# Second products of the feed-forward blocks: three ScalarE casts ordered behind the copy of the first product's bank

## The chip, the cores and the metric

The kernel runs on one core of a Trainium2 chip. The metric is the device time of one execution in microseconds (us); smaller is better. TensorE multiplies, ScalarE and VectorE prepare operands and read results, SyncE issues nearly all transfers, GpSimd does little here. Each engine works through its own list of instructions in the order in which the built program holds them.

## The reference, cut to what matters

Two layers of a streaming-encoder trunk over 256 rows of 1024 channels, in float32. Each layer is a feed-forward block, a mixer (a convolution in the first layer, latent attention in the second) and another feed-forward block, so there are four feed-forward blocks in all:

```python
def swiglu_ffn(h, w1, w3, w2):
    return (jax.nn.silu(h @ w1) * (h @ w3)) @ w2

for i in range(DEPTH):                       # 2 layers, D_FF = 2816
    h = h + 0.5 * swiglu_ffn(rmsnorm(h, ffn_norm1[i]), ffn1_w1[i], ffn1_w3[i], ffn1_w2[i])
    m = rmsnorm(h, mix_norm[i])
    ...
    h = h + 0.5 * swiglu_ffn(rmsnorm(h, ffn_norm2[i]), ffn2_w1[i], ffn2_w3[i], ffn2_w2[i])
```

The change touches only the last product of each block, (...) @ w2, called the down product here.

## The kernel before

**Split operands.** Every float32 operand of a matmul is split in two: a high part, which is ScalarE's cast of the value to the format fp32r, and a low part, which is VectorE's subtraction value minus high part. `mm3` (L330 to L336) makes one product of three matmuls: high times low weight (L332), high times high (L335) and low times high (L336). In the profile a matmul `o<-lo,Gh` is that of L332, `o<-hi,Gl` that of L336.

**Up and gate.** A feed-forward block (`ffn_in`, L834) runs six chunks of the 2816 hidden columns, five of 512 and a sixth of 256. For each chunk and each half of the rows (`tb` 0 and 1) ScalarE computes silu (L948), VectorE multiplies with the other product (L950), and `turn` (L838) brings the gate into transposed form: VectorE transposes 32x32 squares (L470), SyncE writes them to DRAM in four transfers (L474, `gd<-gt`) and reads them back (L479, `gb<-gd`), ScalarE casts them into `Gh` and VectorE subtracts into `Gl` (both L845). `turn` keeps each pair of cast and subtraction in the list `gates`, two pairs a chunk. The first two chunks' gates are read back into the tile `rows4`, since their sums are needed too.

**Seven products in place of eight.** The first 1024 of the hidden columns are multiplied by a scheme that needs seven block products instead of eight (`seven_products`, L366). It wants four sums of row blocks and seven combinations of weight blocks. `sums_of_rows` (L338) makes the sums in `rows4`; `forms_of` (L352) splits each sum into a high part (ScalarE, L361) and a low part (VectorE, L362). The first sum's parts (`s1h`, `s1l`) are made early, ahead of the last chunk; the other three are made when the down product begins (L955), and their parts lie in the space of the block's input (tiles `Xh` and `Xl`, in the profile `rows<-rows`). `load_seven` (L189) makes the weight combinations: differences of raw blocks on VectorE (L200, `raw<-raw,raw`), ScalarE casts (L214) and VectorE subtractions (L200, `lo<-raw,hi`), the last two in halves of 1024 columns.

The products are called P1 to P7 here, each of 12 matmuls:

| product | rows | into bank | waits for |
|---|---|---|---|
| P1 | gate rows | c11 | weights |
| P2 | sum 0 (`s1h`, `s1l`) | c22 | weights |
| P3 | sum 1 | c21, which holds a copy of c11 after P1 | the copy (L383, ScalarE `o<-o`) |
| P4 | gate rows | c11 | weights |
| P5 | sum 2 | c21 | the addition c12 = c21 + kept (L388, VectorE `o<-o,p`), which reads c21 after P3 |
| P6 | sum 3 | c12 | weights |
| P7 | gate rows | c21 | the second addition, c22 = c21 + kept (L395) |

`kept` is ScalarE's copy of c22 after P2 (L386, in the profile `p<-o`). Copies and additions pass through `urgent`, so that in the profile they all stand at L258. P7's weights need a weight difference (`raw<-raw,raw`) that `load_seven` puts behind P5's parts, then a cast, then a subtraction.

**What sets the order.** The instructions are not placed by hand: a scheduler at build time puts them in order, engine by engine, by the position in the program, by priority (`urgent` raises it), by the dependencies of tiles, and by a model of when each could run. `order(ins, first)` (L154) adds an edge between two instructions: `ins` stands behind `first`. L389 to L392 and L396 use it already for the last chunk's gates and for two weight subtractions. When `seven_products` runs for the down product, `gates` ends with the two pairs of the sixth chunk (256 columns); the entry before them is the second half of the fifth chunk.

In the first feed-forward block ScalarE also makes the diagonals of the coming convolution (L1667, `rows<-dpair,wpair`); they are written over `rows4` and so wait until the sums there have been split.

The four down products are called stages A, B, C and D here: A ends the first feed-forward block (126 to 147 us), B the second (399 to 415), C the third (576 to 592), D the fourth (842 to 858).

Of the kernel before, what the change touches and what calls it, by code (L numbers as in the profile page):

```python
# [22 lines left out]
NT = S // P  # L23
# [66 lines left out]
def trunk(ctx: ExitStack, tc: tile.TileContext, x, xt, first, pos, invf, gfin, wdw,  # L90
          f1w13, f1w2, f2w13, f2w2, cw1, cw2, wa, wuq, wukv, wo, wpair, out):
    nc = tc.nc
# [12 lines left out]
    def uid(s):  # L105
        n_uid[0] += 1
        return f"{s}_{n_uid[0]}"
# [9 lines left out]
    def seven(four):  # L117

        group = {}
        return [("seven", j, four, group) for j in range(7)]  # L120
# [33 lines left out]
    def order(ins, first):  # L154
        tc.add_manual_dep(ins.ins, first.name, mybir.DependencyInfo(
            mybir.DependencyClass.NoSync, mybir.DependencyReason.DATA), reason="order")
# [95 lines left out]
    def urgent(f):  # L252

        def g(*args, **kw):
            traced = nc.cur_bb.bb.instructions
            n = len(traced)
            with tc.high_priority():
                r = f(*args, **kw)  # L258
            last = {ins.engine: ins for ins in traced[n:]}
            for engine, ins in last.items():  # L260
                ahead_of.setdefault(engine, []).append(ins)
            return r
        return g

    def load_ahead(ahead=W_BUFS - 2):
        load_to(min(len(blocks), n_used[0] + ahead))
# [5 lines left out]
    def weights(n=1, more=True):  # L272
        out = []
        for _ in range(n):
            n_used[0] += 1
            if more:
                load_ahead()
            else:
                load_ahead(0)
            out.append(loaded[n_used[0] - 1])  # L280
        return out
# [48 lines left out]
    def mm3(o, ah, al, bh, bl, start, stop, after=(), seeded=False):  # L330

        mm = nc.tensor.matmul(o, ah, bl, start=start, stop=False, skip_group_check=seeded)  # L332
        for a in after:
            order(mm, a.ins)
        nc.tensor.matmul(o, ah, bh, start=False, stop=False, skip_group_check=seeded)  # L335
        return nc.tensor.matmul(o, al, bh, start=False, stop=stop, skip_group_check=seeded)  # L336

    def sums_of_rows(x11, x12, x21, x22):  # L338


        sums = [(0, x22, x21, x22, ALU.add), (2, x21, x11, x21, ALU.subtract), (1, x11, x22, x11, ALU.subtract),
                (3, x12, x12, x11, ALU.subtract)]
        for n, out, left, right, op in sums:
            nc.vector.tensor_tensor(out, left, right, op=op)
        return sorted(((n, out) for n, out, *_ in sums), key=lambda s: s[0])

    def whole_rows(xh, xl):
        x = rawp.tile([P, HB], F32, tag="raw", name=uid("xs")).rearrange("p (k t) -> p k t", t=S)
        nc.vector.tensor_add(x, xh.bitcast(F32), xl.bitcast(F32))
        return [x[:, 4 * a:4 * a + 4, tbs(tb)] for tb in range(2) for a in range(2)]  # L350

    def forms_of(sums, sh, sl):  # L352
        sh, sl = (z.rearrange("p k t -> p (k t)").rearrange("p (n c) -> p n c", c=512) for z in (sh, sl))
        out = {}
        for i, (n, x) in enumerate(sums):
            if len(x.shape) == 2:
                high, low = (z[:, i].rearrange("p (t i q) -> p t i q", t=4, q=32) for z in (sh, sl))
                x = x.rearrange("p (i t q) -> p t i q", i=4, q=32)
            else:
                high, low = (z[:, i].rearrange("p (k t) -> p k t", t=P) for z in (sh, sl))  # L360
            nc.scalar.copy(high, x)  # L361
            nc.vector.tensor_sub(low, x, high.bitcast(F32))  # L362
            out[n] = [z[:, i].rearrange("p (k t) -> p k t", t=P) for z in (sh, sl)]
        return out

    def seven_products(xh, xl, forms, banks):  # L366


        def rows(a, tb):
            k = slice(4 * a, 4 * a + 4)  # L370
            return xh[:, k, tbs(tb)], xl[:, k, tbs(tb)]

        def product(a, b, fresh):
            load_ahead(W_BUFS - 1)
            (hi, lo), = weights(1, False)
            for k in range(4):
                c = slice(k * 512, k * 512 + 512)
                mm3(b, a[0][:, k], a[1][:, k], hi[:, c], lo[:, c], fresh and k == 0, k == 3, (), True)

        n0 = n_used[0]  # L380
        c11, c21, c12, c22 = banks[0, 0], banks[1, 0], banks[0, 1], banks[1, 1]
        product(rows(0, 0), c11, True)
        urgent(nc.scalar.copy)(c21, c11)  # L383
        product(forms[0], c22, True)
        kept = tmp.tile([P, 512], F32, tag="s", name=uid("p5"))
        last = urgent(nc.scalar.copy)(kept, c22)  # L386
        product(forms[1], c21, False)
        add = urgent(nc.vector.tensor_add)(c12, c21, kept)  # L388
        order(casts[n0 + 5, 0][1], add.ins)  # L389
        for high, low in gates[-NT:]:  # L390
            order(high, last.ins)
            order(low, add.ins)  # L392
        product(rows(1, 0), c11, False)
        product(forms[2], c21, False)
        add = urgent(nc.vector.tensor_add)(c22, c21, kept)  # L395
        order(casts[n0 + 6, 0][1], add.ins)  # L396
        product(forms[3], c12, False)
        product(rows(1, 1), c21, False)
# [8 lines left out]
    def tbs(tb):  # L407
        return slice(tb * P, (tb + 1) * P)
# [336 lines left out]
    class Rows:  # L745
# [3 lines left out]
                                                      ((0, 0), (0, 1), (1, 0), (1, 1)))}  # L749
            self.seeded = seeded  # L750

        def seven(self, forms):
            seven_products(self.zh, self.zl, forms, self.o)

        def mm(self, part, i, tb, d, o, f0, f1, o0=0, o1=512, after=(), after_last=()):
            hi, lo = part
# [69 lines left out]
    gates = []  # L826

    def ffn(X, make_next, beside=lambda: None, apart=False):
        n = n_ffns[0]
        n_ffns[0] += 1  # L830
        with tc.tile_pool(name=uid("ffn"), bufs=1) as act:
            return ffn_in(act, X, make_next, beside, apart, SEVEN_UP.get(n, ()), n in SEVEN_DOWN)

    def ffn_in(act, X, make_next, beside, apart, seven_up, seven_down):  # L834
        first_form = {}
# [40 lines left out]
        for c in range(6):  # L876

            both = c == 5
# [5 lines left out]
            if seven_up and c == min(seven_up) - (1 if X.whole else 2):  # L884
                forms = forms_of(sums_of_rows(*whole_rows(X.xh, X.xl)), Gh[:, 14:], Gl[:, 14:])
            if c in seven_up:
                for key in ((0, 0), (0, 1), (1, 1), (1, 0)):
                    u[key] = bank("A", "u")
                seven_products(X.xh, X.xl, forms, {(tb, m): b for (m, tb), b in u.items()})
                beside()  # L890
                beside()
            if both and seven_down:
                z11, z21, z12, z22 = (rows4[:, n, :] for n in range(4))
                down_sums = sums_of_rows(z11, z12, z21, z22)
                first_form = forms_of(down_sums[:1], *(act.tile([P, 2, S], F32R, tag=tag, name=uid(tag))
                                                       for tag in ("s1h", "s1l")))
# [55 lines left out]
        o = Rows(Gh, Gl, NF, make_next is Final, seven_down)  # L952
        if seven_down:
            both = (xp.tile([P, KT, S], F32R, tag=tag, name=uid("rows")) for tag in ("Xh", "Xl"))
            o.seven({**first_form, **forms_of(down_sums[1:], *both)})  # L955
        stage.append("down")
        for i in range(4 if seven_down else 0, NF // 2 - (3 if apart else 2)):
            beside()
# [717 lines left out]
    class Rows512:  # L1676

        n = {"ht": 0, "hb": 0}
# [128 lines left out]
```

## Time and profile before

| what | value |
|---|---|
| median of 3 runs | 900.82 us (898.79 to 901.63) |
| the profiled execution's own time | 902.66 us |
| its span (first to last instruction) | 900.9 us |
| granted TensorE clock over it | 0.998 |
| TensorE busy | 890.0 us, 99% of the span |
| VectorE busy | 743.2 us, 83% |
| ScalarE busy | 571.8 us, 63% |

A row of a timeline gives the start in us from the start of the span, the duration, the engine, the line, the operation with out<-in, its shape and count; in brackets stands the idle time of the engine just before it and what ended that. A row of waits gives the engine and its line, what it waited for, the total in us, how often, and the longest. TensorE's matmuls overlap: one is shown as 0.39 us long, while the next starts before it has ended.

### The profile page before, as it was taken

Reading aid. Unit: us, or ns where it says so; the run is one execution under the profiler, and the core shown is the slowest. Engines: PE = TensorE matmul, PEld = TensorE weight load, DVE = VectorE, ACT = ScalarE, POOL = GpSimd, SP = SyncE. Lnnn points to the kernel's source line nnn. Section 1 sums busy time; section 2 is a strip of 40 time slices with the busy share of each in tenths; the row PEclk is TensorE's granted clock in tenths of the full one; section 3 lists DMA queues with packets and bytes.
Section 4 is the critical chain, followed back from the end, with each engine's and each line's share of the span. In section 5 each row is a group of like instructions: output and inputs, shape, how many; then the busy total and the mean of one; then the engine's idle time right before and its main releaser. Section 6 shows DMA issues by size and latency. Waiting matters only on the chain.

```text
span 900.9 us, 12238 instructions
## 1 busy us (share of the span) xinstructions
PE 890.0 (99%) x4221; PEld 745.7 (83%) x4221; DVE 743.2 (83%) x1083; ACT 571.8 (63%) x993; POOL 104.9 (12%) x227
## 2 busy tenths in 40 slices
PE   9999999999999999999999999999999999999997
PEld 7888887898988888878888888788899888888886
DVE  6787779579998998899588989994768579999963
ACT  7966468388877645666375566564767576374752
POOL 1000000069962000000010000000400010000000
PEclk9999999999999999999999999999999999999999
DMA  9987629734315864939759369396545449377451
GB/s 333 363 313 282 212 69 335 295 125 171 105 57 207 291 241 154 368 98 356 283 167 331 136 206 354 98 384 219 198 165 178 150 141 352 99 287 293 169 200 47
DMA packets 71054, 198.94 MB, mean 221 GB/s; under 512 B 12368, under 2 KB 41936, under 8 KB 51664
## 3 DMA queue, kind: packets, MB, share of 16 engines
q1 hardware_dynamic: 70560, 197.47, 61.2%
q8 instruction: 33, 0.54, 0.2%
q10 hardware_dynamic: 432, 0.69, 0.2%
q14 instruction: 29, 0.24, 0.1%
HBM read 181.87 MB, written 16.25 MB: 220 GB/s over the span
## 4 chain that ended last, share of the span: by engine, by line
PE 82%; DVE 7%; DMA 6%; ACT 2%; issue 2%; SPq 0%; POOL 0%; DVEq 0%; ACTq 0%
PE u L336 13%; PE u L332 13%; PE u L335 13%; PE o L332 8%; PE o L336 8%; PE o L335 8%; PE u L993 3%; PE gate L993 3%; DVE lo L200 3%; DMA raw<-in_f1w 2%; PE u L403 2%; PE o L1229 2%; DMA raw<-in_f2w 2%; DVE raw L200 2%; DMA gd<-gt 1%
## 5 line engine op out<-in xcount | busy, mean ns | idle before, releaser
L247 DVE TENSOR_TENSOR lo<-raw,hi 128x1024 fp32r<-128x1024 f32 (+1 forms) x236 | 276.5, 1213 | 41.7 <-ACT hi L246 40.4
L246 ACT CAST hi<-raw 128x1024 fp32r<-128x1024 f32 (+1 forms) x238 | 236.5, 1044 | 89.1 <-DMA raw<-in_f2w 25.1
L332 PE MATMUL u<-lo,Xh 128*128 128x512 f32 x612 | 238.9, 390 | 0.3
L335 PE MATMUL u<-hi,Xh 128*128 128x512 f32 x612 | 238.4, 390 | 0.0
L336 PE MATMUL u<-hi,Xl 128*128 128x512 f32 x612 | 238.2, 390 | 0.0
L332 PEld LDWEIGHTS u<-lo,Xh 128*128 128x128 f32 x612 | 115.0, 188 | 25.3 <-DVE lo L200 1.6
L336 PEld LDWEIGHTS u<-hi,Xl 128*128 128x128 f32 x612 | 115.0, 188 | 24.5 <-DVE Xl L457 0.4
L335 PEld LDWEIGHTS u<-hi,Xh 128*128 128x128 f32 x612 | 115.0, 188 | 23.7
L214 ACT CAST hi<-raw 128x1024 fp32r<-128x1024 f32 x98 | 97.8, 1051 | 53.3 <-DVE raw L200 44.8
L200 DVE TENSOR_TENSOR lo<-raw,hi 128x1024 fp32r<-128x1024 f32 x98 | 116.0, 1217 | 6.4 <-ACT hi L214 6.3
L332 PE MATMUL o<-lo,Gh 128*128 128x512 f32 (+1 forms) x276 | 106.5, 388 | 0.4 <-DVE lo L200 0.4
L335 PE MATMUL o<-hi,Gh 128*128 128x512 f32 (+1 forms) x276 | 106.7, 387 | 0.0
L336 PE MATMUL o<-hi,Gl 128*128 128x512 f32 (+1 forms) x276 | 106.5, 386 | 0.0
L429 POOL TENSOR_TENSOR ms<-ss 128x1 f32<-128x1 f32 x16 | 8.1, 510 | 603.9 <-ACT junk L421 603.9
L200 DVE TENSOR_TENSOR raw<-raw,raw 128x2048 f32<-128x2048 f32 x28 | 63.8, 2280 | 3.9 <-DMA raw<-in_f2w 1.9
L332 PEld LDWEIGHTS o<-lo,Gh 128*128 128x128 f32 x276 | 51.9, 188 | 11.6 <-DVE lo L200 1.3
L336 PEld LDWEIGHTS o<-hi,Gl 128*128 128x128 f32 x276 | 51.9, 188 | 10.5
L335 PEld LDWEIGHTS o<-hi,Gh 128*128 128x128 f32 x276 | 51.9, 188 | 10.3
L1082 DVE SCALAR_TENSOR_TENSOR acc<-V,dw,acc 128x128 f32<-128x128 f32 (+1 forms) x174 | 53.9, 392 | 0.0
L1103 ACT ACTIVATE prod<-V,dw 128x128 f32<-128x128 f32 (+1 forms) x128 | 45.5, 415 | 1.8 <-POOL Y L1104 1.0
L845 ACT CAST Gh<-gb 128x512 fp32r<-128x512 f32 (+1 forms) x32 | 18.1, 567 | 39.2 <-DMA gb<-gd 39.2
L789 DVE SCALAR_TENSOR_TENSOR h<-o,rh,h 128x512 f32<-128x512 f32 (+1 forms) x18 | 12.9, 719 | 29.6 <-PE o L336 29.6
(265 smaller groups left out, 1274.6 us busy)
## 6 DMA issues: line engine op xcount, KB each, us to landing
raw<-in_f2w SPq DMA_DIRECT2D x66, 1024.0 KB, 6.3
raw<-in_f1w SPq DMA_DIRECT2D x62, 1024.0 KB, 6.6
raw<-in_cw SPq DMA_DIRECT2D x12, 1024.0 KB, 5.0
gd<-gt SPq DMA_DIRECT2D x160, 64.0 KB, 3.0
gb<-gd SPq DMA_DIRECT2D x24, 256.0 KB, 2.8
rows<-gd SPq DMA_DIRECT2D x16, 256.0 KB, 4.7
raw<-in_wo SPq DMA_DIRECT2D x4, 1024.0 KB, 4.8
hd<-rows SPq DMA_DIRECT2D x56, 64.0 KB, 2.2
```

The costliest lines, as they stand in the source:

```text
L200: ins = nc.vector.tensor_sub(out, left, right)
L214: casts[n, i] = nc.scalar.copy(hi[:, c], raw[:, c]), sub(lo[:, c], raw[:, c], hi[:, c].bitcast(F32))
L246: casts[len(loaded), i] = (nc.scalar.copy(hi[:, c], raw[:, c]), low.tensor_sub(lo[:, c], raw[:, c], hi[:, c].bitcast(F32)))
L247: low.tensor_sub(lo[:, c], raw[:, c], hi[:, c].bitcast(F32)))
L332: mm = nc.tensor.matmul(o, ah, bl, start=start, stop=False, skip_group_check=seeded)
L335: nc.tensor.matmul(o, ah, bh, start=False, stop=False, skip_group_check=seeded)
L336: return nc.tensor.matmul(o, al, bh, start=False, stop=stop, skip_group_check=seeded)
L403: mm = nc.tensor.matmul(o, al if kind == "x" else ah, bl if kind == "l" else bh, start=start and n == 0, stop=stop and n == len(kinds) - 1)
L845: gates.append((nc.scalar.copy(gh, bv), nc.vector.tensor_sub(low, bv, gh.bitcast(F32))))
L993: mm = nc.tensor.matmul(u[:, t], w[:, c], X.x[:, k, t], start=(k == 0), stop=(k == KT - 1))
L1082: dve_last.append(nc.vector.scalar_tensor_tensor(out if j == j1 - 1 else y, v, w, y, op0=ALU.mult, op1=ALU.add))
L1103: prods_last.append(nc.scalar.activation(p, v, AF.Copy, scale=w))
```

## The change

Three ScalarE casts of each down product get an `order` edge behind the copy c21 <- c11 (`first`): the high parts of sums 2 and 3 (the dictionary `late` carries the two instructions from `forms_of` to `seven_products`) and the high part of the fifth chunk's second gate half (`gates[-NT - 1][0]`). Sum 1's cast is left as it was. The seven products of the up side call `seven_products` without `late`, and nothing is added there.

```diff
-    def forms_of(sums, sh, sl):
+    def forms_of(sums, sh, sl, late={}):
...
-            nc.scalar.copy(high, x)
+            cast = nc.scalar.copy(high, x)
+            if n in late:
+                late[n] = cast
             nc.vector.tensor_sub(low, x, high.bitcast(F32))
...
-    def seven_products(xh, xl, forms, banks):
+    def seven_products(xh, xl, forms, banks, late={}):
...
         product(rows(0, 0), c11, True)
-        urgent(nc.scalar.copy)(c21, c11)
+        first = urgent(nc.scalar.copy)(c21, c11)
+        for cast in [*late.values(), gates[-NT - 1][0]] if late else ():
+            order(cast, first.ins)
         product(forms[0], c22, True)
...
-        def seven(self, forms):
-            seven_products(self.zh, self.zl, forms, self.o)
+        def seven(self, forms, late):
+            seven_products(self.zh, self.zl, forms, self.o, late)
...
-            o.seven({**first_form, **forms_of(down_sums[1:], *both)})
+            late = {2: None, 3: None}
+            o.seven({**first_form, **forms_of(down_sums[1:], *both, late)}, late)
```

The scheduler rebuilds the whole order from this. In the built program the lists differ in these places, the same in B, C and D:

- ScalarE, before: casts of sums 1, 2, 3; silu of the sixth chunk's second half; cast of the fifth chunk's gate; copy c21 <- c11. After: cast of sum 1; silu; copy; gate cast; casts of sums 2 and 3. The cast of the sixth chunk's second gate half moves from behind the casts of the next ordinary weights to a place ahead of the casts of P7's weights.
- VectorE, before: low parts of sums 1, 2, 3; multiplication; subtraction of the gate; first half of P5's low weights; transpose; second half; addition for P5. After: low part of sum 1; multiplication; subtraction of the gate; low parts of sums 2 and 3; transpose; both halves of P5's low weights; first half of P6's low weights; addition for P5; subtraction of the sixth chunk's first gate; second half of P6's; weight difference for P7; subtraction of the sixth chunk's second gate; second addition.
- TensorE, before: P3, P4, P5. After: the first two matmuls of P3, all twelve of P4, the other ten of P3, then P5.

In A TensorE's order is unchanged. ScalarE's list there was: gate cast, casts of sums 1 to 3, silu, 8 diagonals, copy, P5's weight casts, 12 diagonals, copy to `kept`, first half of P6's cast, a gate cast, second half, 4 diagonals, a gate cast, P7's casts. After it is: cast of sum 1, silu, 8 diagonals, copy, gate cast, casts of sums 2 and 3, P5's weight casts, copy to `kept`, P6's casts, 5 diagonals, a gate cast, 5 diagonals, a gate cast, 6 diagonals, P7's casts. VectorE's list in A changes only in where the gate's subtraction and the low parts of sums 2 and 3 stand (behind the sixth chunk's multiplications and transposes), and P6's second half goes ahead of a gate's subtraction.

GpSimd's list is unchanged. SyncE's is unchanged but for one read back of rows between the second and the third block, which is issued before the next four writes and not behind them.

## Prediction

> **What bounds the kernel now.** The page's list of busy times came first, then TensorE's waits over the whole span.
>
> ```profile
> PE 890.0 (99%) x4221; PEld 745.7 (83%) x4221; DVE 743.2 (83%) x1083; ACT 571.8 (63%) x993; POOL 104.9 (12%) x227
> ```
>
> ```profile
> PE o L332 <- ACT o L258: 1.6, 2, 1.2
> PE o L332 <- DVE lo L200: 1.2, 4, 0.4
> ...
> PE o L332 <- DVE o L258: 0.3, 1, 0.3
> ```
>
> TensorE is busy 99% of the span, so the time moves only where a matmul starts sooner or later. All its waits on ScalarE's copy (L258) come to 1.6 us in two places, on weight subtractions to 1.2 us in four, on an addition to 0.3 us. Next I read the timelines of the engines in the four stages. TensorE in B, the first matmul of each product but for the first row, which is P2's last:
>
> ```profile
> 399.72 0.39 PE L336 MATMUL o<-hi,s1l 128*128 128x512 f32 x1
> 401.35 0.50 PE L332 MATMUL o<-lo,rows 128*128 128x512 f32 x1 [1.24 <-ACT o L258]
> ...
> 404.22 0.39 PE L332 MATMUL o<-lo,Gh 128*128 128x512 f32 x1
> ...
> 406.94 0.39 PE L332 MATMUL o<-lo,rows 128*128 128x512 f32 x1
> ...
> 410.01 0.47 PE L332 MATMUL o<-lo,rows 128*128 128x512 f32 x1 [0.19 <-DVE lo L200]
> ...
> 412.82 0.47 PE L332 MATMUL o<-lo,Gh 128*128 128x512 f32 x1
> ```
>
> P4 to P5 is 12 matmuls in 2.72 us: 0.227 each, a product 2.72. P3 was due at 399.72 + 0.23 = 399.95 and began 1.40 late; it then took 2.87, 0.15 over: what TensorE pays to restart (0.09 after P6's shorter wait). P6 was due at 409.66 and came 0.35 late.
>
> ScalarE in B:
>
> ```profile
> 398.27 1.67 ACT L361 CAST rows<-rows 128x512 fp32r<-128x512 f32 x3
> 399.83 0.48 ACT L948 ACTIVATE s<-u,R 128x256 f32<-128x256 f32 x1
> 400.19 0.62 ACT L845 CAST Gh<-gb 128x512 fp32r<-128x512 f32 x1
> 400.70 0.59 ACT L258 COPY o<-o 128x512 f32<-128x512 f32 x1
> 401.22 2.01 ACT L214 CAST hi<-raw 128x1024 fp32r<-128x1024 f32 x2
> 403.11 0.59 ACT L258 COPY p<-o 128x512 f32<-128x512 f32 x1
> 403.59 0.42 ACT L845 CAST Gh<-gb 128x256 fp32r<-128x256 f32 x1
> ```
>
> The copy that P3 wants stands fifth in a row without a gap, though P1 was over by 397.4 (P2's 12 matmuls back from 399.95 is 397.23, plus the tail of 0.16).
>
> **The change, part by part.** *What it removes in B and C.* By the starts above a sum's cast takes 0.52, silu 0.36, the gate cast 0.51, the copy 0.52. Behind one cast and silu the copy starts at 398.27 + 0.52 + 0.36 = 399.15 and ends at 399.74, before P3's 399.95. That is worth 1.40 + 0.15 = 1.55 in B. The five instructions come to the same sum, so from 401.22 on ScalarE stands as before. C:
>
> ```profile
> 577.21 0.50 PE L332 MATMUL o<-lo,rows 128*128 128x512 f32 x1 [0.38 <-ACT o L258]
> ```
>
> ```profile
> 576.03 1.89 DVE L362 TENSOR_TENSOR rows<-rows,rows 128x512 fp32r<-128x512 f32 x3
> ```
>
> A wait is counted from the last matmul's end, 0.16 behind the next one's due time, so P3 was due at 577.21 - 0.38 - 0.16 = 576.67: worth 0.54 + 0.15 = 0.69. In D it removes nothing:
>
> ```profile
> 842.84 0.39 PE L332 MATMUL o<-lo,rows 128*128 128x512 f32 x1
> ```
>
> ```profile
> 840.87 1.89 DVE L362 TENSOR_TENSOR rows<-rows,rows 128x512 fp32r<-128x512 f32 x3
> ```
>
> *What it adds in B, C, D.* The built order puts P4 into P3, with ten of P3's matmuls behind it. P4 was the cover of the addition that P5 waits for: P3 ended 2.72 us before P5 in B, and the addition fits into that. Now P5 follows P3's last matmul directly, and VectorE has more ahead of the addition: a second low half. VectorE in B:
>
> ```profile
> 400.17 1.89 DVE L362 TENSOR_TENSOR rows<-rows,rows 128x512 fp32r<-128x512 f32 x3
> 401.98 0.42 DVE L950 TENSOR_TENSOR s<-s,u 128x256 f32<-128x256 f32 x1
> 402.31 0.69 DVE L845 TENSOR_TENSOR Gl<-gb,Gh 128x512 fp32r<-128x512 f32 x1
> 402.91 1.22 DVE L200 TENSOR_TENSOR lo<-raw,hi 128x1024 fp32r<-128x1024 f32 x1
> 404.05 0.44 DVE L470 STREAM_TRANSPOSE gt<-s 128x256 f32<-128x256 f32 x1
> ...
> 405.51 0.69 DVE L258 TENSOR_TENSOR o<-o,p 128x512 f32<-128x512 f32 x1
> 406.12 0.41 DVE L845 TENSOR_TENSOR Gl<-gb,Gh 128x256 fp32r<-128x256 f32 x1
> 406.44 2.29 DVE L200 TENSOR_TENSOR raw<-raw,raw 128x2048 f32<-128x2048 f32 x1
> ```
>
> Start to start: low part 0.60, multiplication 0.33, gate 0.60, weight half 1.14, transpose 0.36, addition 0.61, small gate 0.32, difference 2.20. In the new order the addition may start 0.60 + 0.33 + 0.60 + 1.20 + 0.36 + 3 x 1.14 = 6.51 after the low parts begin: 406.68 in B, 582.54 in C, 847.38 in D. P3's last matmul ends 23 x 0.227 + 0.39 = 5.60 after P3's due time: 405.55, 582.27, 848.44. The later of the two decides: VectorE in B and C, TensorE in D. P5 follows the addition's start by 0.69 and a hand-over of 0.06, against a due time of P3's plus 24 x 0.227 = 5.44:
>
> - B: 407.43 against 405.39, 2.04 late, with restart 2.19; less the 1.55 removed, +0.64.
> - C: 583.29 against 582.11, 1.18, with restart 1.33; less 0.69, +0.64.
> - D: 849.24 against 848.28, 0.96, with restart 1.11; nothing to take off, +1.11.
>
> Behind the addition nothing of P5 itself is late. P6's first half is now made ahead of the addition, so the old waits at P6 go: 0.44 in B, by the four waits on L200 as much in C, none in D. P7 pays instead: from the addition's start VectorE needs 0.61 + 0.32 + 1.14 + 2.29 = 4.36 to the end of the weight difference, then ScalarE's cast of a half (1.0, half of 2.01) and VectorE's half (1.22), with 0.2 of hand-overs 6.8 in all; TensorE reaches P7 0.75 + 0.15 + 5.44 = 6.34 after that start. So about 0.5 late plus restart, 0.6 in each of the three (B and C had a restart of 0.1 there). Sums: B 0.64 - 0.44 + 0.5 = +0.7, C the same, D +1.7: **+3.1**.
>
> *What it removes in A.* TensorE's order stays, and these are its first matmuls of P3, P5, P6, P7:
>
> ```profile
> 130.98 0.45 PE L332 MATMUL o<-lo,rows 128*128 128x512 f32 x1
> ...
> 136.94 0.50 PE L332 MATMUL o<-lo,rows 128*128 128x512 f32 x1 [0.27 <-DVE o L258]
> ...
> 140.35 0.47 PE L332 MATMUL o<-lo,rows 128*128 128x512 f32 x1 [0.40 <-DVE lo L200]
> ...
> 143.80 0.50 PE L332 MATMUL o<-lo,Gh 128*128 128x512 f32 x1 [0.41 <-DVE lo L200]
> ```
>
> ```profile
> 128.37 2.02 ACT L1667 ACTIVATE rows<-dpair,wpair 128x64 f32<-128x64 f32 x8
> 130.29 0.58 ACT L258 COPY o<-o 128x512 f32<-128x512 f32 x1
> 130.80 1.99 ACT L214 CAST hi<-raw 128x1024 fp32r<-128x1024 f32 x2
> 132.70 2.98 ACT L1667 ACTIVATE rows<-dpair,wpair 128x64 f32<-128x64 f32 x12
> 135.58 0.57 ACT L258 COPY p<-o 128x512 f32<-128x512 f32 x1
> ```
>
> P7 was due at 130.98 + 48 x 0.227 = 141.86 and came at 143.80: 1.94 lost. The root is `kept`, held to 135.58 behind twelve diagonals, which also holds the addition, the weight difference behind it, and so P6 and P7. The new list has those twelve behind `kept` and P6's casts. Counted forward: P1 began at 130.98 - 5.44 = 125.54, and the last up matmul, whose operand's space the sums' parts take, ends 0.16 behind; cast 0.6 and low part 0.7 give 127.0, when the eight diagonals may overwrite sum 1. Then the copy at 129.0, gate cast, two sum casts and P5's casts to 133.0, `kept` done 133.6; the addition near 134.5, the difference at 137.3, P6's half at 138.5 against a due 139.14. P7's casts now stand behind all 16 diagonals and two gate casts, 135.4 + 16 x 0.25 + 0.6 = 140.0; cast 1.0 and subtraction 1.22 give 142.2 with 0.3 late and a restart. I take **-1.65**. Bounds: -2.05 if P7 finds its weights, -1.0 if a gate's read back holds the casts half a microsecond.
>
> *The rest.* ScalarE's and VectorE's durations stay. SyncE's read between two blocks only moves ahead of writes that wait for a later transpose: nothing.
>
> Sum: -1.65 + 3.1 = **+1.45 us**. The profiled execution's 902.66 would become 904.1. Its span of 900.9 has 1.8 around it; the median, 900.82, lies 1.84 under that execution, and 900.82 + 1.45 = **902.3**.
>
> **The rivals.** *The second small gate stops ScalarE.* Its cast moves ahead of P7's casts, and it needs a transfer that shares the engines with weight loads:
>
> ```profile
> 407.81 0.34 SPq L479 DMA_DIRECT2D gb<-gd  x1
> ```
>
> ```profile
> DMA to landing us min/median/max: 2.0/2.5/4.3
> ```
>
> With the longest landing that is 412.1. The transpose starts about 1.1 sooner (402.90 for 404.05), so I expect 411.0, level with the difference's end (406.68 + 4.36 = 411.04). It decides once it lands later than that. With no gain in issue, ScalarE stands 1.1 plus 0.31 for the cast in B, and some 1.0 in C, 0 in D: +2.3 on the sum, 904.6, a slowdown. Against it: writes and read follow the earlier transpose.
>
> *A's gain is swallowed later.* VectorE is busy 83% and near full in the convolution; if it and not TensorE paces that, A gives 0 and the sum is +3.1, 903.9. Against it: the waits show TensorE waiting almost nowhere.
>
> *The copy simply comes sooner.* Without new waits at P5 and P7 the gain is all of the losses counted: 1.55 + 0.44 + 0.69 + 0.44 + 2.05 = 5.2, 895.6. It speaks against this that matmuls stand in one list, and P5 needs the bank that the addition reads. The edges do what they say either way; the copy is ahead in all four built lists.
>
> *The clock.* TensorE idles up to 1.24 us now, and the next matmuls come at the full 0.227. In the new B it would idle 2.04 - 0.16 = 1.9. If that dropped the clock to half for the 24 matmuls of P5 and P6, 5.44 us more would fall in B: 907.7. I give it 2%.
> The Trainium skill (page "TensorE: Matmul & The Clock Gate", section "What's actually happening") lets the clock fall to half only after an idle window of about 3.4 us. By that rule none of these waits does it; the trace agrees as far as 1.24 us.
>
> **How the numbers follow.** Forecast 0.60; gate 0.17; swallowed 0.13; copy alone 0.08; clock 0.02. No change is within 0.3%, 2.7 us, about what a measurement of this kernel can tell. The forecast's own range is A's bounds (-2.05 to -1.0) with half a microsecond either way at each of B, C and D: 900.4 to 904.4. With the gate and the swallowed gain, which both lie over 2.7, and the runs' spread, the range is 899.6 to 905.3. Faster is the copy alone, 0.08. Slower is gate, swallowed and clock, 0.32. Same is the rest, 0.60.
>
> **What would show it.** Right: in B, C, D no wait on ScalarE's copy, and at P5 a wait of TensorE on VectorE's addition (1.9, 1.0, 0.8 from the last matmul's end); a wait at P7 on L200 in each; P7 in A near 142.2. Wrong: P5 without a wait; ScalarE standing before L845 in B or C for a read back; a lower granted clock; A's P7 still at 143.8.

## The result, and the profile after

| | before | after |
|---|---|---|
| median, 11 runs each on one chip | 901.63 us (898.79 to 903.86) | 904.24 us (902.31 to 905.97) |
| ratio of the two, 95% interval | | 1.0031 (1.0019 to 1.0044) |
| the profiled execution | 902.66 us, span 900.9 | 904.33 us, span 902.5 |
| granted clock | 0.998 | 0.998 |

The changed kernel is slower, by 2.8 us by the ratio (1.7 to 4.0 by its interval) and by 1.7 between the two profiled executions. That lies at the bound of 2.7 us up to which the prediction spoke of no change.

TensorE's waits over the whole span of the changed kernel (its engine and line, what it waited for, total in us, times, longest):

```profile
PE o L332 <- DVE o L258: 4.2, 3, 1.8
PE warm L324 <- DVE still L319: 1.0, 1, 1.0
PE o L332 <- DVE lo L200: 0.8, 3, 0.3
PE u L332 <- DVE lo L247: 0.5, 1, 0.5
PE u L407 <- ACT Xh L636: 0.2, 1, 0.2
```

The wait on ScalarE's copy (1.6 us in two places before) is gone. In its place stand three waits on VectorE's addition, 4.2 us, and three on a weight subtraction, 0.8. The other rows stand outside the four stages, at 1.0, 28.1 and 6.9 us. Next comes TensorE's timeline in B. The line numbers of the changed kernel stand two to five higher than before behind L361; P3's and P4's first and last matmuls are shown, then the two matmuls with a wait, each behind the last matmul before it:

```profile
398.12 0.39 PE L336 MATMUL o<-hi,s1l 128*128 128x512 f32 x1
398.34 0.39 PE L332 MATMUL o<-lo,rows 128*128 128x512 f32 x1
398.57 0.39 PE L335 MATMUL o<-hi,rows 128*128 128x512 f32 x1
...
401.29 0.39 PE L336 MATMUL o<-hi,Gl 128*128 128x512 f32 x1
401.51 0.39 PE L336 MATMUL o<-hi,rows 128*128 128x512 f32 x1
...
403.56 0.39 PE L336 MATMUL o<-hi,rows 128*128 128x512 f32 x1
405.70 0.47 PE L332 MATMUL o<-lo,rows 128*128 128x512 f32 x1 [1.75 <-DVE o L258]
...
411.04 0.39 PE L336 MATMUL o<-hi,rows 128*128 128x512 f32 x1
411.67 0.50 PE L332 MATMUL o<-lo,Gh 128*128 128x512 f32 x1 [0.24 <-DVE lo L200]
```

P3 starts at 398.34, without a gap behind P2; two of its matmuls, then P4, then ten more, as the built order had it. All of the idle time now stands at P5 (1.75) and at P7 (0.24). The same two places in C and in D:

```profile
582.61 0.47 PE L332 MATMUL o<-lo,rows 128*128 128x512 f32 x1 [1.57 <-DVE o L258]
...
588.57 0.50 PE L332 MATMUL o<-lo,Gh 128*128 128x512 f32 x1 [0.26 <-DVE lo L200]
```

```profile
849.30 0.47 PE L332 MATMUL o<-lo,rows 128*128 128x512 f32 x1 [0.88 <-DVE o L258]
855.26 0.50 PE L332 MATMUL o<-lo,Gh 128*128 128x512 f32 x1 [0.27 <-DVE lo L200]
```

VectorE in B shows why the addition is late:

```profile
397.94 0.68 DVE L364 TENSOR_TENSOR rows<-rows,rows 128x512 fp32r<-128x512 f32 x1
...
401.04 2.31 DVE L200 TENSOR_TENSOR lo<-raw,hi 128x1024 fp32r<-128x1024 f32 x2
403.72 1.23 DVE L200 TENSOR_TENSOR lo<-raw,hi 128x1024 fp32r<-128x1024 f32 x1 [0.36 <-ACT hi L214]
404.86 0.69 DVE L258 TENSOR_TENSOR o<-o,p 128x512 f32<-128x512 f32 x1
405.46 0.42 DVE L849 TENSOR_TENSOR Gl<-gb,Gh 128x256 fp32r<-128x256 f32 x1
405.79 1.22 DVE L200 TENSOR_TENSOR lo<-raw,hi 128x1024 fp32r<-128x1024 f32 x1
406.93 2.29 DVE L200 TENSOR_TENSOR raw<-raw,raw 128x2048 f32<-128x2048 f32 x1
409.13 0.42 DVE L849 TENSOR_TENSOR Gl<-gb,Gh 128x256 fp32r<-128x256 f32 x1
409.47 0.69 DVE L258 TENSOR_TENSOR o<-o,p 128x512 f32<-128x512 f32 x1
410.39 2.36 DVE L200 TENSOR_TENSOR lo<-raw,hi 128x1024 fp32r<-128x1024 f32 x2 [0.23 <-ACT hi L214]
```

Call the start of sum 1's low part T (397.94 here, 400.17 before). The addition starts at T + 6.92; before it was T + 5.34. VectorE now stands idle twice for ScalarE, 0.36 ahead of P6's half and 0.23 ahead of P7's. ScalarE's casts of P6's two halves:

```profile
401.67 2.01 ACT L214 CAST hi<-raw 128x1024 fp32r<-128x1024 f32 x2
```

VectorE goes on at 403.72, as the second of these casts has ended (403.68). So the half ahead of the addition is P6's second one: an edge that both kernels have, `order(casts[n0 + 5, 0][1], add.ins)` (L389 before), keeps the first behind the addition. The prediction took it for the first. ScalarE ahead of P7's half:

```profile
408.53 0.41 ACT L849 CAST Gh<-gb 128x256 fp32r<-128x256 f32 x1 [4.85 <-DMA gb<-gd]
409.30 2.01 ACT L214 CAST hi<-raw 128x1024 fp32r<-128x1024 f32 x2 [0.36 <-DVE raw L200]
```

The small gate's cast ended at 408.94, and ScalarE then still waited for the weight difference: the gate did not hold it up, with 0.36 us to spare (0.20 in C, 0.94 in D). In A, ScalarE's list did what it was forecast to do:

```profile
127.51 2.03 ACT L1672 ACTIVATE rows<-dpair,wpair 128x64 f32<-128x64 f32 x8 [0.39 <-DVE rows L364]
129.44 0.57 ACT L258 COPY o<-o 128x512 f32<-128x512 f32 x1
...
133.42 0.57 ACT L258 COPY p<-o 128x512 f32<-128x512 f32 x1
...
140.25 1.99 ACT L214 CAST hi<-raw 128x1024 fp32r<-128x1024 f32 x2
```

`kept` starts at 133.42 in place of 135.58, and P7 follows at 142.60, 0.35 behind P6's last matmul, where it came at 143.80 before:

```profile
142.25 0.39 PE L336 MATMUL o<-hi,rows 128*128 128x512 f32 x1
142.60 0.50 PE L332 MATMUL o<-lo,Gh 128*128 128x512 f32 x1
```

**A measure for the stages.** From the timelines of each profile I take the time from P1's first matmul to P7's first (16.32 if TensorE never waits: six products of 2.72), and the time from T to P7's first.

| kernel | P1 to P7: A | B | C | D | T to P7: B | C | D |
|---|---|---|---|---|---|---|---|
| before | 18.26 | 18.31 | 17.44 | 16.32 | 12.65 | 12.64 | 12.85 |
| after | 16.44 | 18.77 | 18.57 | 17.88 | 13.73 | 13.72 | 14.38 |
| change | -1.82 | +0.46 | +1.13 | +1.56 | +1.08 | +1.08 | +1.53 |

The stages together give +1.33. The rest of the +1.6 in span lies outside: P1 of A starts 0.62 later (126.16 for 125.54), behind the two waits at 6.9 and 28.1 us (0.23 and 0.53), which the profile of before doesn't have, and the stretch from A's P7 to B's P1 makes up 0.41 (a wait of 0.39 at 264 us in the profile of before is missing here). No edge of the change stands at these places, and what brings these waits isn't known.

Two things were open after this. Is A's gain real at the end? And what was the copy's wait worth: if splitting P3 is undone, does B give back the 1.55 that the prediction counted for it?

### The profile page after: what moved, and what is told of

Same layout as the page of the kernel before. It is cut to its first block, busy times and chain, and to the rows that moved or that the text cites. A ratio compares the mean times of both kernels' runs of the same rounds, so it can differ in the third digit from the quotient of the medians.

```text
span 902.5 us, 12240 instructions
## 1 busy us (share of the span) xinstructions
PE 889.4 (99%) x4221; PEld 744.8 (83%) x4221; DVE 743.9 (82%) x1083; ACT 571.5 (63%) x993; POOL 105.5 (12%) x227
## 4 chain that ended last, share of the span: by engine, by line
PE 66%; DVE 15%; DMA 8%; ACT 5%; issue 2%; SPq 1%; POOL 0%; DVEq 0%; ACTq 0%
PE u L332 10%; PE u L336 10%; PE u L335 10%; PE o L332 8%; PE o L336 8%; PE o L335 8%; DVE lo L247 3%; DVE lo L200 3%; DMA gd<-gt 3%; DVE acc L1087 3%; ACT hi L214 2%; PE u L998 2%; PE gate L998 2%; DMA raw<-in_f2w 2%; DVE raw L200 2%
```

## The experiments

Each was timed against the kernel before on the same chip; diffs are against the changed kernel unless said otherwise.

**1. Edges in the first block only.**

```diff
-            late = {2: None, 3: None}
+            late = {2: None, 3: None} if n_ffns[0] == 1 else {}
```

> The three edges only in stage A; B, C and D are built as before. Theory (the split of P3 costs, A gains): in A P5, P6 and P7 start without the waits of 0.27, 0.40 and 0.41, P7 starts 16.4 us behind P1 for 18.26 before, and the gain of 1.8 us reaches the end: 0.2% faster than before, span about 899.1. Rival (A's gain is swallowed in the convolution): the same P7, but the stages behind start where they did and the time is that of before within 0.5 us.

Measured: 899.99 us against 901.56, ratio 0.9983 (0.9970 to 0.9996), span 900.2. P1 to P7 in A takes 16.45. A's gain arrives at the end: -1.5 us by the ratio (-2.7 to -0.4 by its interval), where the stage had -1.8. The stretch from A's P7 to B's P1, with the convolution in it, takes 250.99 us here and 250.71 before. So at most 0.3 of the 1.8 is lost there, and that all of it is swallowed is refuted.

**2. Edges in the other three blocks only.**

```diff
-            late = {2: None, 3: None}
+            late = {2: None, 3: None} if n_ffns[0] > 1 else {}
```

> The three edges only in stages B, C and D; A is built as before. Theory: waits at P5 of 1.75, 1.57 and 0.88 and at P7 of about 0.25 each; P1 to P7 longer by 0.5 in B, 1.1 in C, 1.6 in D: 3.2 us over before, 0.35% slower, and slower than with all four. Rival (A is what slows the kernel, or nothing but noise does): within 0.5 us of before.

Measured: 905.02 us, ratio 1.0034 (1.0021 to 1.0048), +3.1 us; span 903.6. A is as before (18.28); B, C and D take 19.19, 17.90 and 17.89, together 2.91 over the profile of before. The sum is as expected, its division is not: the waits at P5 are 2.19, 0.88 and 0.88, where the changed kernel had 1.75, 1.57 and 0.88. Experiments 1 and 2 split the change into a gain of one and a half and a loss of three.

**3. The split of P3 undone.** All edges stay; P4's matmuls are put behind P3's last.

```diff
-        def product(a, b, fresh):
+        def product(a, b, fresh, behind_mm=()):
...
-                mm3(b, a[0][:, k], a[1][:, k], hi[:, c], lo[:, c], fresh and k == 0, k == 3, (), True)
+                mm = mm3(b, a[0][:, k], a[1][:, k], hi[:, c], lo[:, c], fresh and k == 0, k == 3, behind_mm, True)
+            return mm
...
-        product(forms[1], c21, False)
+        third = product(forms[1], c21, False)
...
-        product(rows(1, 0), c11, False)
+        product(rows(1, 0), c11, False, (third,) if late else ())
```

With it TensorE's order is that of before, and so are VectorE's order of P6's and P7's weights and the place of the small gate's cast.

> All four stages changed, and P4's matmuls stand behind P3's last, so that TensorE keeps its order of before. Theory (only the split of P3 costs, the early copy is a gain): no wait on the copy, no wait at P5, the waits at P6 of about 0.2 as before; B shorter than before by 1.5, C by 0.7, D the same, A by 1.8: 4.0 us or 0.45% faster than before. Rival (the casts of sums 2 and 3 and of the gate, and the low parts behind them, come too late for P5 whatever TensorE's order): P5 still waits about 1 us in B and C, and the time is that of before or more.

Measured: 900.59 us, ratio 0.9985 (0.9972 to 0.9998), -1.35; span 900.8. My own number, -4.0, missed. P1 to P7 takes 16.45, 18.63, 17.05 and 16.54. The loss of B to D is gone (+0.32, -0.39 and +0.22 against before), but the early copy paid nothing on top, though P3 now begins only 0.13 late in B. TensorE's rows with a wait in B, and P7's first matmul:

```profile
399.37 0.50 PE L336 MATMUL o<-hi,rows 128*128 128x512 f32 x1 [0.39 <-DVE rows L364]
...
408.47 0.47 PE L332 MATMUL o<-lo,rows 128*128 128x512 f32 x1 [0.73 <-DVE lo L200]
...
411.31 0.44 PE L332 MATMUL o<-lo,Gh 128*128 128x512 f32 x1
```

The first row is P3's third matmul: it needs the low part of sum 1, which VectorE ends at 399.31, and so it waits for T itself. VectorE's row of T in that profile, with the work ahead of it:

```profile
394.12 4.59 DVE L200 TENSOR_TENSOR lo<-raw,hi 128x1024 fp32r<-128x1024 f32 x4
398.63 0.68 DVE L364 TENSOR_TENSOR rows<-rows,rows 128x512 fp32r<-128x512 f32 x1
```

P7 comes at 411.31 - 398.63 = 12.68 behind T, and in C and D 12.64: the kernel before had 12.65 and 12.64 in B and C, with the copy's wait. Experiment 1, whose B, C and D have the old order, has 12.68, 12.67 and 12.68. VectorE of the kernel before, behind the rows shown in the prediction:

```profile
408.64 2.36 DVE L200 TENSOR_TENSOR lo<-raw,hi 128x1024 fp32r<-128x1024 f32 x2
410.91 0.70 DVE L258 TENSOR_TENSOR o<-o,p 128x512 f32<-128x512 f32 x1
411.51 2.35 DVE L200 TENSOR_TENSOR lo<-raw,hi 128x1024 fp32r<-128x1024 f32 x2
```

From T to here VectorE has no gap at all. So the new theory: from T on, VectorE's unbroken work sets P7, whatever TensorE waits for earlier. What is taken off the copy's wait is waited out later instead, here 0.39 us at P3's third matmul and 0.73 at P6. The fifteen instructions from T to the first half of P7's weights add up to it, start to start: 3 x 0.60, 0.33, 0.60, 2 x 1.14, 0.36, 0.61, 0.32, 2.20, 2.27, 0.60 and 1.18 are 12.55, and 0.1 for the hand-over.

**4. P6's second half put behind the addition.** In the changed kernel an edge in each of the four stages puts VectorE's subtraction for that half behind the addition that P5 waits for.

```diff
+        if late:
+            order(casts[n0 + 5, 1][1], add.ins)
```

> TensorE's order as in the changed kernel; both halves of P6's low weights stand behind the addition that P5 waits for, on VectorE. Theory (VectorE's chain of addition, P6's weights, weight difference and P7's weights is the bound once P4 no longer covers it): P5's wait falls to about 0.9 in B and C and stays in D, but P7's grows from 0.25 to about 1.3 in all three, so the time is 0.5 to 1.5 us over the changed kernel's. Rival (the half of P6's weights ahead of the addition is a loss by itself): B and C gain 0.8 each, P7 keeps its 0.25, 1.6 us under the changed kernel's.

Measured: 905.91 us, ratio 1.0042 (1.0029 to 1.0056); span 904.3. TensorE in B:

```profile
404.55 0.50 PE L332 MATMUL o<-lo,rows 128*128 128x512 f32 x1 [0.86 <-DVE o L258]
...
411.75 0.50 PE L332 MATMUL o<-lo,Gh 128*128 128x512 f32 x1 [1.46 <-DVE lo L200]
```

The wait at P5 halves (1.75 to 0.86), the one at P7 grows from 0.24 to 1.46. C and D have the same two waits, and P1 to P7 takes 19.10, 19.09 and 19.10 in B, C and D, 2.07 together over the changed kernel. VectorE's addition in B:

```profile
403.80 0.70 DVE L258 TENSOR_TENSOR o<-o,p 128x512 f32<-128x512 f32 x1 [0.43 <-PE o L336]
```

Here VectorE has a gap: the addition waits 0.43 us for P3's last matmul (1.01 in C, 1.26 in D). So T no longer sets P7 (T to P7 is 13.81, 14.37 and 14.63), but P3's end does, by one and the same distance. The 0.86 at P5 is the wait that the split brings by itself, without a weight half ahead of the addition. Putting that half behind it shortens P5's wait and lengthens P7's by more.

**5. A shorter chain, tried with GpSimd.** In the kernel before (no edges), the low parts of sums 2 and 3 go to GpSimd, which is to take 1.2 us out of VectorE's work behind T.

```diff
-    def forms_of(sums, sh, sl):
+    def forms_of(sums, sh, sl, late=()):
...
-            nc.vector.tensor_sub(low, x, high.bitcast(F32))
+            (nc.gpsimd if n in late else nc.vector).tensor_sub(low, x, high.bitcast(F32))
...
-            o.seven({**first_form, **forms_of(down_sums[1:], *both)})
+            o.seven({**first_form, **forms_of(down_sums[1:], *both, (2, 3))})
```

> The kernel before, with the low parts of sums 2 and 3 on GpSimd in place of VectorE, in all four stages; no edge of the change. New theory (in B, C and D P6 and P7 are paced by VectorE, P7 12.65 us after it begins sum 1's low part; the copy's wait only hides under that): VectorE's chain is 1.2 shorter, P7 at most 11.5 behind it, so that now the copy's wait of about 1.3 in B and 0.6 in C is what is left; P7 late by 1.4 to 1.6 in B and 0.6 to 0.9 in C for 2.0 and 1.1: about 0.8 us under before. First theory (the copy's wait paces B and C): as before within 0.4 us.

Measured: 905.67 us against 902.66, ratio 1.0030 (1.0015 to 1.0044): slower, a miss. VectorE in B:

```profile
400.72 1.75 DVE L362 TENSOR_TENSOR rows<-rows,rows 128x512 fp32r<-128x512 f32 x1
...
402.73 1.46 DVE L845 TENSOR_TENSOR Gl<-gb,Gh 128x512 fp32r<-128x512 f32 x1
```

GpSimd beside it:

```profile
400.04 3.61 POOL L362 TENSOR_TENSOR rows<-rows,rows 128x512 fp32r<-128x512 f32 x2 [114.59 <-PE o L336]
```

VectorE's two subtractions, 0.69 each by themselves, take 1.75 and 1.46 while GpSimd subtracts. That is 1.83 more, against 1.2 taken away, and the chain grew by 0.7: 13.33, 13.34 and 13.32 in B, C and D. The edit failed as a shortening, yet P7 again follows T by one constant. P1 to P7 took 19.05, 19.68, 17.38 and 18.16 in A to D. In A the list of diagonals changed as well (14 ahead of the copy), and T moved against P1: 0.7 later than before in B, 0.8 sooner in C, 1.4 later in D. So the total is not a price of GpSimd alone.

**6. The same on GpSimd, with the edges and P3 whole (experiment 3).**

> The change with P4 kept behind P3, and the low parts of sums 2 and 3 on GpSimd. New theory (VectorE's chain is the bound behind the copy): with both taken off, P7 in B late by 0.4 to 0.8 and not at all in C and D, against 2.0, 1.1 and 0 before and 2.3, 0.7 and 0.2 with the edges alone: with A's 1.8 about 4 us or 0.45% under before, and 2.5 us under the kernel that only keeps P4 behind P3. First theory (VectorE does not pace these stages): as that kernel, 1 us under before.

Measured: 903.48 us against 902.66, ratio 1.0003 (0.9991 to 1.0015): a miss as well, since a gain of 4 us was expected. T to P7 is 13.20, 13.19, 13.16: 0.5 over experiment 3. Beside GpSimd VectorE's subtraction of the gate took 1.62 in B, and its two weight halves 3.09 in place of 2.32.

**7. A shorter chain without GpSimd, and the copy's wait left in.** In the kernel before, two subtractions of gates that only the work behind P7 needs (the fifth chunk's second half, the sixth chunk's first) are put behind P7's weights (a third buffer for the gates read back makes that possible). By the rows of before this takes 0.60 + 0.32 out of VectorE's work behind T: 11.73.

```diff
-    def seven_products(xh, xl, forms, banks):
+    def seven_products(xh, xl, forms, banks, late=()):
...
-            b = pool.tile([P, 512], F32, tag=tag + "b", name=uid(tag + "b"), bufs=2)
+            b = pool.tile([P, 512], F32, tag=tag + "b", name=uid(tag + "b"), bufs=3 if tag == "g" else 2)
...
+        if late:
+            for low in (gates[-NT - 1][1], gates[-NT][1]):
+                order(low, casts[n0 + 6, 1][1].ins)
...
-            seven_products(self.zh, self.zl, forms, self.o)
+            seven_products(self.zh, self.zl, forms, self.o, (1,))
```

> The kernel before without the edges of the change; on VectorE the subtractions of the fifth chunk's second gate half (0.60) and of the sixth chunk's first (0.32) stand behind P7's low weights, with a third buffer for read back gates so that no transfer waits for them. VectorE theory: P6 comes 8.9 us after sum 1's low part begins where nothing else holds it, P7 11.7 (9.84 and 12.65 before); in B the copy's wait of about 1.3 plus restart is then what is left, P7 late by 1.5 (2.0 before), in C by 0.7 to 0.9 (1.1). Theory that the copy's wait paces B and C: P7 late as before. A's list of diagonals changes too, with P3 late there by 1 to 2.

Measured once: 903.26 us, beside 903.27. TensorE's one wait in B:

```profile
402.77 0.50 PE L332 MATMUL o<-lo,rows 128*128 128x512 f32 x1 [1.19 <-ACT o L258]
```

P3 is 1.35 late for the copy, and P7 1.49, the copy's wait and the restart and nothing more. Here, with the chain short enough, the copy does set the end of B. T to P7 is 12.18, 12.19 and 12.57, longer than the chain's 11.73, as it must be where TensorE sets P7. The stages B, C, D gained 0.50, 1.03 and 0; C's P7 is 0.09 late for 0.7 to 0.9 expected, and its gain isn't the chain's alone, since T came 0.58 sooner against P1 and no matmul waited for the copy. A lost 0.60, with 16 diagonals ahead of the copy.

**8. Both: edges, P3 whole, and the two subtractions deferred.**

> The change with P4 kept behind P3, and the same two subtractions behind P7's low weights. VectorE theory: with the copy early and VectorE's chain 0.92 shorter, P7 comes 11.7 us after sum 1's low part begins in B (late by 1.0 to 1.4, 2.3 with the edges alone), and is on time in C and D: 1.8 us under the kernel that only keeps P4 behind P3, 2.8 us or 0.3% under before. Theory that something other than VectorE's chain holds P6 and P7: P7 late by 2.3, 0.7 and 0.2 as in that kernel, 1 us under before.

Measured: 901.24 us against 903.27, ratio 0.9975 (0.9963 to 0.9987), -2.3 us. This beats both kernels; from the plain experiments 1 and 3 its interval doesn't part it. T to P7 is 11.74, 11.72 and 11.77, against 11.73 worked out. VectorE in C:

```profile
574.72 0.68 DVE L364 TENSOR_TENSOR rows<-rows,rows 128x512 fp32r<-128x512 f32 x1
...
587.40 1.02 DVE L853 TENSOR_TENSOR Gl<-gb,Gh 128x512 fp32r<-128x512 f32 x2
```

The deferred work stands at 587.40, behind P7's weights, and P7 in C is 0.21 late where it was 1.12. A, B, C and D gained 1.83, 0.43, 0.91 and nothing, 3.2 together. In this profile none of that is left at the end: its span is 900.9, as before (its time of 902.70 us is the longest of the twelve, whose median is 901.24). Outside P1 to P7, TensorE has these waits that the profile of before doesn't have, 2.2 us in all:

```profile
PE u L332 <- DVE lo L200: 1.0, 2, 0.7
PE o L332 <- DVE lo L247: 0.7, 4, 0.2
PE u L411 <- ACT Xh L640: 0.5, 1, 0.5
```

The 0.7 us of the second row stand right behind P7 in the four stages, where VectorE makes up for the deferred subtractions. The 1.0 of the first row stands at 799 and 801 us, ahead of D, where experiment 3 has 1.5 and the kernel before nothing; why is open. The 0.5 of the third stands at 5.3 us. For the rest of the 3.2 no wait shows.

## Why the prediction was right, and where it wasn't

**The time.** Forecast 902.3, measured 904.24, inside the range. The forecast's step was +1.45; the four stages show +1.33, the profile +1.6 to +1.7, experiments 1 and 2 together +1.6, and the runs +2.8 with 1.7 as the lower bound, so by the ratio the step was forecast too small. Of the 1.9 between forecast and median, 0.8 is the kernel before itself, whose median over 11 runs is 901.63 and not 900.82. What the rest is, the runs do not settle.

**A, -1.65 forecast, -1.82 measured.** The mechanism held in each step: `kept` at 7.26 behind P1 (forecast 7.5), P7's casts at 14.09 behind P1 (forecast 14.5), no wait at P5 and P6, a small one at P7. "A's gain is swallowed later", as a whole, fell with experiment 1.

**The split of P3.** P5's wait appeared in all three blocks: 1.75, 1.57 and 0.88 against 1.9, 1.0 and 0.8. D, where nothing was to be removed, came to +1.56 (+1.7 forecast). The cause is shown by experiment 3, which undoes the split and loses all three waits on the addition. With the split the scheduler also puts VectorE's order of P6's and P7's weights back; experiment 4 tells the two apart, since it keeps the split, puts P6's half back, and has a wait of 0.86 in all three blocks.

**C's size.** "In the new order the addition may start ... 6.51 after the low parts begin" was short by 0.41. The half of P6's weights ahead of the addition is one for which VectorE waited 0.36 for ScalarE's cast; the sum had counted VectorE's own work and no cast. That is most of the 1.57 for 1.0 in C. In B it was covered up by T, which came 0.63 sooner against P3's due time than before (-0.41 for +0.22). What moves T isn't known: VectorE had no gap ahead of it, and over the profiles it lies between -0.41 and +0.91 in B.

**The step that was wrong though the sum came out.** "That is worth 1.55 in B", and 0.69 in C, for the copy's wait. It was worth nothing: experiment 3 has the copy in time, in B but for 0.13, and P7 at T + 12.68 in B and T + 12.64 in C, where the kernel before had it at T + 12.65 and T + 12.64. (C is 0.39 shorter there since T came 0.39 sooner against P1.) The prediction priced the copy by TensorE's lost time and put the waits at P6 aside as 0.44. Those waits were VectorE's chain catching up, and a gain at P3 comes back as waits behind it. P3 itself could not have run through either: its third matmul, due at 400.40 in B, needs the low part of sum 1, which began at 400.17 and takes 0.69. That the old waits at P6 go was forecast for a wrong reason too: P6's first half still stands behind the addition, and P6 doesn't wait since P5 is later itself. The right account for B and C is the chain's growth by 1.08: 0.40 more for two weight halves ahead of the addition (403.72 - 401.04 = 2.68 for 2.28), 0.34 for the second small gate, now ahead of P7's weights, and 0.32 from the second addition to P7's weights (0.92 for 0.60), since P6's halves no longer cover ScalarE's cast of P7's; 0.02 is left. In D, where TensorE set P7 before, the addition waited for P3's end as well (start at T + 7.57), and P7 came at T + 14.38. The net of the wrong route agreed, since it took off a gain that was not there and added waits at P5 (2.19 and 1.33) that contained the same time. That B and C came out near +0.7 (+0.46 and +1.13) is luck to that extent.

**P7's new wait.** Forecast 0.5 and the restart, measured 0.24 to 0.27 and the restart.

**The rivals.** The gate landed in time in B, C and D; in B its read back was issued 1.3 sooner relative to T and took 4.2 us to land, in C and D 4.6 and 4.5, over the 4.3 that the prediction took for the longest. "The copy simply comes sooner" fell with the waits at P5, and experiment 3 shows that without them, too, the early copy gains nothing in B (18.63 for 18.31). The clock stayed:

```profile
405.70:416.00 10.30, 10.06 (x43) 7.97 (x44) 10.07 (x10) 7.11 (x9) 0.00 (x0) 1.00 0.94 358
```

This is the row of the changed kernel's windows behind the longest wait (the stretch, then busy us and counts of TensorE, its weight loads, VectorE, ScalarE and GpSimd, the granted clock, the DMA engines' busy share and GB/s): 1.00 after 1.75 us of idle time.

**Still open.** Why the scheduler splits P3 when the casts are ordered was read from its output only. Whether experiment 8 is better than experiment 3 isn't parted by the runs.

## What to carry to other kernels

An edge that is meant for one queue lets a scheduler reorder the others: look at the built order of every engine before pricing it, and ask what the moved work was covering. A removed wait is worth only what the next bound leaves of it; that bound is found by measuring from one event on the suspected engine to the end of the stage in two kernels, and if this distance stays while the wait goes (12.65 here), the wait was not the bound. The distance speaks only while that engine has no gap in between, as experiment 4 shows. Here, putting work that is needed late behind the chain shortened it by 0.9, and spreading the work over a second engine lengthened it by 0.5 to 0.7.

## What the hardware showed that was not expected

A subtraction on GpSimd holds up VectorE's. A 128x512 subtraction of two inputs takes 0.69 us on VectorE alone, and took 1.46 to 1.75 in experiment 5 while GpSimd ran a subtraction of the same shape; GpSimd's own eight there took 13.6 us, 1.7 each:

```profile
L362 POOL TENSOR_TENSOR rows<-rows,rows 128x512 fp32r<-128x512 f32 x8 | 13.6, 1718 | 444.2 <-ACT rows L361 329.6 <-PE o L336 114.6
```

The Trainium skill (page "SBUF — State Buffer", section "Who interferes with whom") says that a VectorE instruction with two inputs in SBUF contends with a GpSimd instruction that reads SBUF. The trace agrees, and puts 0.8 to 1.1 us on VectorE's instruction; how long GpSimd's takes alone no run here shows.

TensorE pays a little to start again: behind the 1.75 us wait its first two matmuls come 0.30 and 0.24 apart where 0.227 is usual (405.70, 406.00, 406.24), and by P6 the product is 0.12 late.
